# An RWKV block cut into 37 paced steps in place of 31, and eight small predicated copies into two

## The chip, the cores and the metric

The kernel runs on one core of a Trainium2 chip. What is compared is the device time of one execution in microseconds, the median over several runs. The engines are TensorE (PE, matrix products; its weight loads are listed as PEld), VectorE (DVE), ScalarE (ACT), GpSimd (POOL) and SyncE (SP, which only starts transfers here).

## What is computed

One layer of a hybrid network runs over 2048 prompt rows and 32 sample rows of width 1024: a modulated norm, one projection to 3464 columns, three kinds of heads side by side on those columns, an output projection, and a feed-forward part. All is float32; a large product is made of three products of rounded parts. The change lies in the first kind of heads, RWKV-7, four heads of width 64, whose state S is carried along the rows:

```python
def step(S, inp):
    r_t, k_t, v_t, kk_t, a_t, w_t = inp
    s_kk = jnp.einsum('bhvk,bhk->bhv', S, kk_t)
    S = (S * w_t[:, :, None, :] - s_kk[..., None] * (kk_t * a_t)[:, :, None, :]
         + v_t[..., None] * k_t[:, :, None, :])
    return S, jnp.einsum('bhvk,bhk->bhv', S, r_t)
```

Before it stand elementwise operations on the projected columns (decay w, gate a, a normalized kk); after it come a norm by head, a bonus term and a gate. The other two kinds are HGRN2 (four heads, a gated recurrence) and forgetting attention (eight heads).

## The kernel before

The first part of the program, `project_and_recur` (L1956), does three things at once: the large projection, the RWKV recurrence and the HGRN2 recurrence. The projection is `cm_cols` and `tm_cols` of `InProj`: groups of 24 matmuls into a PSUM tile `ip_p` (L378 to L380, L409 to L411). It does not depend on the recurrences, and it is what PE has to do while they wait for other engines.

The RWKV rows are taken in 16 blocks of 128 rows, and one of 64 for the sample: 17 blocks, each a generator `rwkv_block` (L1097) that yields after each step. A block turns the recurrence into products within chunks of 64 rows. Its steps, with the names that return below:

- loads and token shift, decay and gate (`rw_ga`), the norm of kk by a product with `bones` (L1161, "the bones product") and the operations after it;
- the operands: `G` (L1171 to L1174) and `kb` (L1175 to L1182), eight operations on DVE and one on POOL, all in one step;
- the products of `G` and `kb` (L1189, "the kb product"), masked on DVE into `gm` (L1193), one half copied by ACT into `m0` (L1197);
- the first level of a triangular inverse `tt`: eight predicated copies (L1219, which are recorded at L1015 in the helper `by_level`), a transpose to `tn` (L1220), and in the same step the transpose of v on PE, copied by ACT to `rw_wu` (L1223);
- the product `nv` of `gm` and `rw_wu` (L1229);
- five more levels (h = 2 to 32), each of two half steps: PE, then ACT (`rw_x`, L1258); PE, then DVE (predicated copy, transpose L1267);
- products with the inverse, the two chunk states `rw_s`, the output `rw_y`, its norm, and its store to `yT`, a transfer started from ACT's queue (L1344).

The order of the program's instructions is written by `interleave` (L2105): it always advances the generator with the least position. A block starts every 1.0, and each of its yields moves it on by `RW_LEN / RW_STEPS`. So a step is 1.5/31 = 0.0484 of a block's start distance, and blocks overlap. `coupled` (L2093) advances an HGRN2 block by 0.65 of a step at each RWKV step. The projection's generator advances by its own measure beside them. The products of the two recurrences go through `small` (L222), which puts them ahead of projection matmuls that are ready and fixes their order against them. How many projection matmuls stand on PE between two products of a block is thus set by the number of yields between them. An engine takes its instructions in the order in which they stand.

After the last block the rest of the projection goes on beside attention; the output projection and the feed-forward part follow.

Of the kernel before, what the change touches and what calls it, by code (L numbers as in the profile page):

```python
# [1003 lines left out]
def halves(t, h, u):  # L1004

    return t.rearrange("p (b u x) -> p b u x", u=2, x=h)[:, :, u, :]


def by_level(K, dst, h, src, rows=slice(0, 128)):

    n, b, x = dst.shape[1] // 64, 32 // h, h
    m = K.lev_up[h][rows].bitcast(mybir.dt.uint32).rearrange("p (b x) -> p b x", x=h)
    m = m[:, None, :, :].broadcast_to([m.shape[0], n, b, x])
    d = dst.rearrange("p (c b u x) -> p c b u x", c=n, u=2, x=h)[:, :, :, 1, :]
    K.nc.vector.copy_predicated(d, m, src)  # L1015
# [81 lines left out]
def rwkv_block(K, rp, pp, t0, T, n, first, st):  # L1097
# [5 lines left out]
    NK, W = 2 * C, 2 * T  # L1103
# [33 lines left out]
    for j in range(2):  # L1137
# [5 lines left out]
    sq = tmp()  # L1143
    nc.scalar.activation(sq, kk, AF.Square)
    yield


    b = sb("rw_b")
# [23 lines left out]
    nc.vector.tensor_tensor(G[:, 1], ch(xr), ch(w), ALU.mult)  # L1172
    nc.gpsimd.tensor_tensor(G[:, 2], K.i2[:, None, :].broadcast_to([128, NK, 64]), ends.broadcast_to([128, NK, 64]),
                            ALU.mult)  # L1174
    kb = rp.tile([128, NK, 2, 64], F32, name="rw_kb", bufs=KB)  # L1175
    nc.vector.scalar_tensor_tensor(kk, kk, -1.0, av, ALU.mult, ALU.mult)
    nc.vector.tensor_tensor(kb[:, :, 1, :], ch(kk), ch(wi), ALU.mult)
    kp = av
    for j in range(2):
        nc.vector.tensor_scalar(kp[:, js[j]], av[:, js[j]], vec(K, "rw_k_a", j), K.ka1[:, j:j + 1], ALU.mult, ALU.add)  # L1180
    nc.vector.tensor_tensor(kp, kp, xk, ALU.mult)
    nc.vector.tensor_tensor(kb[:, :, 0, :], ch(kp), ch(wi), ALU.mult)  # L1182

    yield

    gm, gps = [], [pt() for _ in hs]
# [4 lines left out]
    for ps in gps:  # L1191
        g = rp.tile([128, NK, 192], F32, name=f"rw_gm{len(gm)}", bufs=GM)
        nc.vector.tensor_tensor(g[:, :, 0:128], ps[:, :128 * NK].rearrange("p (k x) -> p k x", x=128), mask, ALU.mult)  # L1193
        gm.append(g)
        if len(gm) == 1:
            m0 = rp.tile([64, NK, 64], F32, name="rw_m0", bufs=1)
            nc.scalar.activation(m0, g[64:, :, 0:64], AF.Copy)  # L1197
    yield

    kf = kb.rearrange("p k a t -> p k (a t)")  # L1200
# [3 lines left out]
    tt = rp.tile([128, NK, 64], F32, name="rw_tt", bufs=TT)  # L1204
    tn = rp.tile([128, NK, 64], F32, name="rw_tn", bufs=1)
    wu = rp.tile([128, 2, NK, 2, 64], F32, name="rw_wu", bufs=WU)
    flat = lambda t: t.rearrange("p k t -> p (k t)")

    def tokens(src):

        ps = pt()
        for j in range(2):
            transpose(ps[:T, 128 * j:128 * j + 128], src[:, C * j:C * j + C, :], K.ident)
        return [ps[64 * c:64 * c + 64, :256].rearrange("p (j h x) -> p j h x", j=2, h=2) for c in range(C)]

    nc.gpsimd.tensor_copy(tt, K.i2[:, None, :].broadcast_to([128, NK, 64]))
    for h, m in zip(hs, mt):
        for k in range(NK):
            by_level(K, tt[h, k, :], 1, halves(m[:, k, :], 1, 1)[:, None], h)  # L1219
    nc.vector.transpose(tn, tt)  # L1220

    for c, v in enumerate(tokens(ch(xv))):
        nc.scalar.activation(wu[:64].rearrange("p h (j c) a x -> p c a j h x", j=2)[:, c, 1], v, AF.Copy)  # L1223
    yield

    nv = pt()
# [136 lines left out]
class Rwkv:  # L1363
# [13 lines left out]
    def block(self, t0):  # L1377
        first = 0 if t0 == 0 else None
        return rwkv_block(self.K, self.rp, self.pp, t0, self.T, self.T, first, self.st)
# [16 lines left out]
    def sample(self):  # L1396
        K, rp, pp, nc = self.K, self.rp, self.pp, self.K.nc
        s0 = rp.tile([128, 2, 64], F32, name="rw_z", bufs=1)
        nc.sync.dma_start(out=s0, in_=K.a["state_rwkv"][0, 0].rearrange("(j h) v k -> (h v) j k", j=2))
        ps = pp.tile([128, 512], F32, name="rw_ps")  # L1400
        for p in range(2):
            for h in (slice(0, 64), slice(64, 128)):
                nc.tensor.matmul(ps[h, 64 * p:64 * p + 64], lhsT=s0[h, p, :], rhs=K.i2[h, :], start=True, stop=True)
        s = rp.tile([128, 2, 64], F32, name="rw_zs", bufs=1)
        nc.scalar.activation(s, ps[:, :128].rearrange("p (j x) -> p j x", j=2), AF.Copy)
        st = [s]
        yield from rwkv_block(K, rp, pp, SEQ, 64, NS, 1, st)
        self.out(st[0], K.o["rw_state_sample"])
# [678 lines left out]
        yield from K.fx.run([(h, 0) for h in range(8)], 512, 4, K.banks, FX_LEAD0)  # L2087


RW_LEN, RW_STEPS, HG_STEP, IP_LEAD = 1.5, 31, 0.65, 0.5  # L2090


def coupled(main, other, steps):  # L2093
# [133 lines left out]
```

## Time and profile before

| | |
|---|---|
| median of 3 runs (lowest to highest) | 3648.11 us (3646.69 to 3655.67) |
| profiled execution, its own time | 3646.97 us |
| span of its trace | 3645.3 us |
| PE busy | 3416.8 us, 94% |
| DVE, ACT, POOL busy | 52%, 38%, 38% |
| mean granted TensorE clock | 0.972 |

Busy time counts an engine from an instruction's start to its end. PE is busy nearly always, so what is to be had is in its gaps and in stretches where its clock is granted at less than full speed. The first recurrence product starts at about 168 us, the last at 1254.7 us.

### The profile page before, as it was taken

To read this page: it belongs to the slowest core of one execution; us is meant where nothing else is said; L and a number is where in the kernel's file an instruction comes from. 1 tells how busy PE (TensorE), PEld (TensorE's weight loads), DVE (VectorE), ACT (ScalarE), POOL (GpSimd) and SP (SyncE) were. 2 spreads that over 40 slices of the span, in tenths; PEclk is the share of its full clock that TensorE was granted. 3 is DMA by queue.
4 is the path that set the end of the run, shared out by engine and by line. 5 is a ranking of instruction groups with operands and counts; after the bars stand their busy time and mean duration, and the time that the engine had idled before them with its cause. 6 is when DMAs were issued, how large, how long until landed. Compare 5 with 4: busy or idle time off the path is not lost.

```text
span 3645.3 us, 61001 instructions
## 1 busy us (share of the span) xinstructions
PE 3416.8 (94%) x24106; PEld 2877.2 (79%) x24106; DVE 1890.9 (52%) x3953; ACT 1399.7 (38%) x2865; POOL 1382.2 (38%) x1458
## 2 busy tenths in 40 slices
PE   7998899989899998999999999899999999999999
PEld 5988788878777875666666666688999998998998
DVE  3456656575657565656666665532333344233336
ACT  4345556455455453544443443322122213211212
POOL 5424444443334413644443443333223333322223
PEclk9999999999989998999999999999999999999999
DMA  6433334324542344322222214533222232211212
GB/s 213 144 111 100 93 115 128 122 79 142 173 133 67 119 140 126 122 69 66 60 80 59 75 50 107 178 128 100 64 64 76 70 95 98 70 58 47 70 58 96
DMA packets 362482, 361.25 MB, mean 99 GB/s; under 512 B 35359, under 2 KB 304244, under 8 KB 361140
## 3 DMA queue, kind: packets, MB, share of 16 engines
q1 hardware_dynamic: 324336, 320.02, 28.8%
q10 hardware_dynamic: 37476, 37.29, 3.3%
q8 instruction: 189, 3.10, 0.4%
q14 instruction: 97, 0.79, 0.1%
q0 software_dynamic: 384, 0.05, 0.0%
HBM read 291.14 MB, written 66.14 MB: 98 GB/s over the span
## 4 chain that ended last, share of the span: by engine, by line
PE 58%; DVE 5%; POOL 4%; issue 3%; DMA 2%; ACT 2%; ACTq 0%; POOLq 0%; SPq 0%; DVEq 0%
PE ff_p L1878 8%; PE ff_p L1879 8%; PE ff_p L1877 8%; PE ff_o L1828 4%; PE ff_o L1829 4%; PE ff_o L1827 4%; PE pb_pv L712 4%; PE pb_sc L665 2%; PE pb_ps L728 2%; PE rw_ps L227 2%; POOL fx_acc L722 2%; PE pb_ps L729 1%; PE op_p L1737 1%; PE op_p L1735 1%; PE op_p L1736 1%
## 5 line engine op out<-in xcount | busy, mean ns | idle before, releaser
L1878 PE MATMUL ff_p<-h_lo,wih 128*128 128x384 f32 (+2 forms) x1760 | 622.7, 354 | 0.2 <-POOL h_lo L1952 0.2
L1877 PE MATMUL ff_p<-h_hi,wih 128*128 128x384 f32 (+2 forms) x1760 | 621.2, 353 | 1.1 <-DVE op_r L1739 0.4
L1879 PE MATMUL ff_p<-h_hi,wil 128*128 128x384 f32 (+2 forms) x1760 | 620.9, 353 | 1.1 <-POOL wil L1764 1.1
L1764 POOL TENSOR_TENSOR wil<-ff_st,wih 128x1024 fp32r<-128x1024 f32 x134 | 322.0, 2403 | 578.9 <-ACT wih L1763 540.2
L378 PE MATMUL ip_p<-h_hi,w_hi 128*128 128x256 f32 (+1 forms) x1472 | 458.9, 312 | 19.4 <-ACT ip_e L345 6.6
L379 PE MATMUL ip_p<-h_lo,w_hi 128*128 128x256 f32 (+1 forms) x1472 | 428.9, 292 | 6.7 <-POOL h_lo L203 3.6
L380 PE MATMUL ip_p<-h_hi,w_lo 128*128 128x256 f32 (+1 forms) x1472 | 427.0, 290 | 0.0
L1877 PEld LDWEIGHTS ff_p<-h_hi,wih 128*128 128x128 f32 x1760 | 331.3, 188 | 17.2 <-issue 0.9
L1879 PEld LDWEIGHTS ff_p<-h_hi,wil 128*128 128x128 f32 x1760 | 332.9, 189 | 14.2 <-POOL wil L1764 1.4
L1878 PEld LDWEIGHTS ff_p<-h_lo,wih 128*128 128x128 f32 x1760 | 331.4, 188 | 14.5 <-POOL h_lo L1952 0.6
L378 PEld LDWEIGHTS ip_p<-h_hi,w_hi 128*128 128x128 f32 x1472 | 284.7, 194 | 50.6 <-issue 19.0
L1764 POOL TENSOR_TENSOR wol<-ff_st,woh 128x1024 fp32r<-128x1024 f32 x66 | 161.3, 2449 | 408.0 <-ACT woh L1763 408.0
L722 POOL TENSOR_TENSOR fx_acc<-fx_acc,fx_pt 128x512 f32<-128x512 f32 (+3 forms) x176 | 209.1, 1203 | 274.0 <-PE pb_pv L712 157.1
L1886 DVE TENSOR_TENSOR ff_sg<-ff_sg,ff_p 128x384 f32<-128x384 f32 (+2 forms) x110 | 64.5, 586 | 461.7 <-PE ff_p L1879 457.0
L1833 DVE TENSOR_TENSOR acc<-acc,ff_o 128x512 f32<-128x512 f32 (+1 forms) x306 | 208.8, 684 | 173.6 <-PE ff_o L1829 173.0
L379 PEld LDWEIGHTS ip_p<-h_lo,w_hi 128*128 128x128 f32 x1472 | 286.1, 194 | 14.4 <-POOL h_lo L203 4.7
L1827 PE MATMUL ff_o<-woh,act_h 128*128 128x512 f32 (+1 forms) x724 | 286.9, 396 | 10.3 <-ACT act_h L1887 7.6
L380 PEld LDWEIGHTS ip_p<-h_hi,w_lo 128*128 128x128 f32 x1472 | 285.0, 194 | 3.9 <-issue 2.4
L1829 PE MATMUL ff_o<-woh,act_l 128*128 128x512 f32 (+1 forms) x724 | 287.7, 398 | 0.0
L1828 PE MATMUL ff_o<-wol,act_h 128*128 128x512 f32 (+1 forms) x724 | 286.9, 396 | 0.0
L1763 ACT ACTIVATE wih<-ff_st 128x1024 fp32r<-128x1024 f32 x134 | 142.0, 1060 | 362.4 <-PE ff_p L1878 315.9
L336 POOL TENSOR_TENSOR w_lo<-w_st,w_hi 128x256 fp32r<-128x256 f32 (+2 forms) x220 | 163.2, 771 | 179.8 <-ACT w_hi L334 161.8
(450 smaller groups left out, 7085.7 us busy)
## 6 DMA issues: line engine op xcount, KB each, us to landing
ff_st<-w_ffn_in SPq DMA_DIRECT2D x132, 512.0 KB
w_st<-w_in SPq DMA_DIRECT2D x88, 512.0 KB
ff_st<-w_ffn_out SPq DMA_DIRECT2D x68, 512.0 KB
cm<-ip_e SPq DMA_DIRECT2D x92, 256.0 KB
x_t<-w_ada SPq DMA_DIRECT2D x32, 512.0 KB
fx_kr<-cm SPq DMA_DIRECT2D x80, 128.0 KB
w_st<-w_in SPq DMA_DIRECT2D x16, 520.0 KB
w_a<-w_ada SPq DMA_DIRECT2D x8, 1024.0 KB
```

The source lines that it names most:

```text
L378: nc.tensor.matmul(ps[:, :T], lhsT=whi[:, d, us], rhs=S.hi[:, d, :T], start=(d == 0), stop=False)
L379: nc.tensor.matmul(ps[:, :T], lhsT=whi[:, d, us], rhs=S.lo[:, d, :T], start=False, stop=False)
L380: K.behind[1:] = [nc.tensor.matmul(ps[:, :T], lhsT=wlo[:, d, us], rhs=S.hi[:, d, :T], start=False, stop=(d == ND - 1))]
L722: eng.tensor_tensor(acc[i % 2][:m, c0:nq], acc[i % 2][:m, c0:nq], pt[:m, c0:nq], ALU.add)
L1764: nc.gpsimd.tensor_tensor(lo, st, f32(hi), ALU.subtract)
L1827: nc.tensor.matmul(ps[:m], lhsT=ah[:, js], rhs=wh[:, cs], start=(n == 0), stop=False)
L1828: nc.tensor.matmul(ps[:m], lhsT=ah[:, js], rhs=wl[:, cs], start=False, stop=False)
L1829: nc.tensor.matmul(ps[:m], lhsT=al[:, js], rhs=wh[:, cs], start=False, stop=(n == 1))
L1833: nc.vector.tensor_tensor(acc[j][:m, cs], acc[j][:m, cs], ps[:m], ALU.add)
L1877: nc.tensor.matmul(ps[:, :S], lhsT=w[0][:, ds], rhs=hh[:, d, :S], start=(d == 0), stop=False)
L1878: nc.tensor.matmul(ps[:, :S], lhsT=w[0][:, ds], rhs=hl[:, d, :S], start=False, stop=False)
L1879: nc.tensor.matmul(ps[:, :S], lhsT=w[1][:, ds], rhs=hh[:, d, :S], start=False, stop=(d == ND - 1))
```

## The change

Six more `yield`s are put into `rwkv_block`: an empty step after kk, three between the operands and the kb product (`G` / one half of `kb` / the other half / an empty step), one empty step after `gm`, one after the step with `rw_wu`. The eight predicated copies of the first level, for each half of the partitions one for each of four pieces of 64 columns, become one copy for each half. The pace goes from 31 steps in 1.5 to 37 in 1.6, and HGRN2 advances by 0.6 per step.

```diff
     sq = tmp()
     nc.scalar.activation(sq, kk, AF.Square)
     yield
+    yield
...
     nc.gpsimd.tensor_tensor(G[:, 2], K.i2[:, None, :].broadcast_to([128, NK, 64]), ends.broadcast_to([128, NK, 64]),
                             ALU.mult)
+    yield
     kb = rp.tile([128, NK, 2, 64], F32, name="rw_kb", bufs=KB)
     nc.vector.scalar_tensor_tensor(kk, kk, -1.0, av, ALU.mult, ALU.mult)
     nc.vector.tensor_tensor(kb[:, :, 1, :], ch(kk), ch(wi), ALU.mult)
+    yield
     kp = av
     for j in range(2):
         nc.vector.tensor_scalar(kp[:, js[j]], av[:, js[j]], vec(K, "rw_k_a", j), K.ka1[:, j:j + 1], ALU.mult, ALU.add)
     nc.vector.tensor_tensor(kp, kp, xk, ALU.mult)
     nc.vector.tensor_tensor(kb[:, :, 0, :], ch(kp), ch(wi), ALU.mult)
-
+    yield
     yield
...
             m0 = rp.tile([64, NK, 64], F32, name="rw_m0", bufs=1)
             nc.scalar.activation(m0, g[64:, :, 0:64], AF.Copy)
     yield
+    yield
...
     for h, m in zip(hs, mt):
-        for k in range(NK):
-            by_level(K, tt[h, k, :], 1, halves(m[:, k, :], 1, 1)[:, None], h)
+        by_level(K, flat(tt)[h], 1, m.rearrange("p k (b u x) -> p k b u x", u=2, x=1)[:, :, :, 1, :], h)
     nc.vector.transpose(tn, tt)
 
     for c, v in enumerate(tokens(ch(xv))):
         nc.scalar.activation(wu[:64].rearrange("p h (j c) a x -> p c a j h x", j=2)[:, c, 1], v, AF.Copy)
     yield
+    yield
...
-RW_LEN, RW_STEPS, HG_STEP, IP_LEAD = 1.5, 31, 0.65, 0.5
+RW_LEN, RW_STEPS, HG_STEP, IP_LEAD = 1.6, 37, 0.6, 0.5
```

The change moves instructions on every engine. Two places are shown, both of the 13th block. The first is PE, from the kb product to the product nv. Before, with the last row shown the first nv product:

```order
L227 MATMUL rw_ps<-rw_G,rw_kb 128x128 x8
L227 MATMUL rw_ps<-ident,rw_v 128x128 x2
L378 MATMUL ip_p<-h_hi,w_hi 128x256
L379 MATMUL ip_p<-h_lo,w_hi 128x256
L380 MATMUL ip_p<-h_hi,w_lo 128x256
L195 MATMUL nt_ps<-ident,xn 128x128 x3
L227 MATMUL rw_ps<-rw_wu,rw_gm_13046 64x64
```

Now, in the middle of the same stretch (the transpose of v, between projection matmuls):

```order
L378 MATMUL ip_p<-h_hi,w_hi 128x256
L379 MATMUL ip_p<-h_lo,w_hi 128x256
L380 MATMUL ip_p<-h_hi,w_lo 128x256
L227 MATMUL rw_ps<-ident,rw_v 128x128 x2
L227 MATMUL hg_ps<-hg_x 64x96 x8
L378 MATMUL ip_p<-h_hi,w_hi 128x256
```

From the kb product to the transpose of v there are now 12 projection matmuls (the first three rows shown are the last of them), and from there to nv 12 more. Before there were none and 3, so 24 stand where 3 stood.

The second place is ACT, around the copy of v to `rw_wu`. Before:

```order
L334 ACTIVATE w_hi<-w_st 128x4x256 x2
L1344 DMA yT<-rw_y 128x2x128
L1076 ACTIVATE rl_e<-rl_e,lsc 128x128
L1223 ACTIVATE rw_wu<-rw_ps 64x2x2x64 x2
L1197 ACTIVATE rw_m_13048<-rw_gm_13046 64x256
```

Now (the lines have moved by 3 or 4):

```order
L1348 DMA yT<-rw_y 128x2x128
L345 ACTIVATE ip_e<-ip_p 128x256
L1200 ACTIVATE rw_m_13042<-rw_gm_13040 64x256
L1226 ACTIVATE rw_wu<-rw_ps 64x2x2x64 x2
L201 ACTIVATE h_hi<-h_t 128x4x128
```

The store of the block before, which waits for POOL's `rw_y`, stands ahead of `rw_wu` in both; the copy to `m0` now stands between, and nv is 24 projection matmuls from the kb product in place of 3.

## Rows read from the trace of the kernel before

**Rows 1.** The page's head and its part 1.

```profile
span 3645.3 us, 61001 instructions
...
PE 3416.8 (94%) x24106; PEld 2877.2 (79%) x24106; DVE 1890.9 (52%) x3953; ACT 1399.7 (38%) x2865; POOL 1382.2 (38%) x1458
```

**Rows 2.** Windows, the recurrence stage: busy by engine, granted clock, DMA share, GB/s.

```profile
160.00:1255.00 1095.00, 1005.62 (x11453) 887.34 (x11453) 680.97 (x1913) 575.64 (x1479) 458.99 (x751) 0.96 0.38 115
```

**Rows 3.** Waits of PE, 160 to 1255 us: total us, times, longest.

```profile
PE rw_ps L227 <- DVE rw_kb L1182: 20.3, 14, 3.5
PE rw_ps L227 <- ACT rw_wu L1223: 10.8, 7, 2.4
PE rw_ps L227 <- DVE rw_gm L1193: 10.3, 5, 3.6
...
PE rw_ps L227 <- DVE w_lo L336: 3.7, 1, 3.7
...
PE rw_ps L227 <- DVE rw_tn L1267: 2.3, 2, 2.1
...
PE rw_ps L227 <- ACT rw_x L1258: 2.1, 4, 0.7
```

**Rows 4.** Waits of PE, 160 to 970 us (blocks 1 to 12).

```profile
PE rw_ps L227 <- DVE rw_kb L1182: 15.0, 10, 3.5
```

**Rows 5.** Waits of PE, 970 to 1255 us (blocks 13 to 17).

```profile
PE rw_ps L227 <- DVE rw_kb L1182: 5.3, 4, 3.0
```

**Rows 6.** Windows of 20 us behind seven long waits; the granted clock stands third last.

```profile
322.00:342.00 20.00, 17.55 (x213) 15.97 (x212) 13.77 (x45) 10.60 (x33) 6.44 (x14) 0.91 0.36 93
452.00:472.00 20.00, 17.53 (x160) 16.23 (x161) 9.53 (x39) 7.51 (x32) 5.67 (x22) 0.91 0.26 72
517.00:537.00 20.00, 16.52 (x187) 15.20 (x187) 15.24 (x47) 7.69 (x19) 7.60 (x13) 0.91 0.55 165
860.00:880.00 20.00, 17.06 (x217) 15.13 (x219) 14.46 (x46) 9.02 (x30) 4.88 (x8) 0.91 0.40 117
989.00:1009.00 20.00, 16.41 (x175) 14.60 (x174) 13.35 (x42) 7.17 (x22) 7.61 (x11) 0.66 0.27 81
1056.00:1076.00 20.00, 18.37 (x178) 16.35 (x180) 13.63 (x48) 6.84 (x22) 6.67 (x9) 0.57 0.35 104
1214.00:1234.00 20.00, 17.96 (x212) 15.98 (x213) 8.57 (x31) 7.03 (x25) 2.91 (x3) 0.83 0.19 62
```

**Rows 7.** Timeline of PE around the kb product of block 14: start, us, instruction.

```profile
1054.21 0.28 PE L380 MATMUL ip_p<-h_hi,w_lo 128*128 128x256 f32 x1
1054.33 0.28 PE L378 MATMUL ip_p<-h_hi,w_hi 128*128 128x256 f32 x1
1057.63 2.08 PE L227 MATMUL rw_ps<-rw_G,rw_kb 64*128 64x128 f32 x16 [3.03 <-DVE rw_kb L1182]
...
1060.34 0.41 PE L380 MATMUL ip_p<-h_hi,w_lo 128*128 128x256 f32 x1
1060.56 0.41 PE L378 MATMUL ip_p<-h_hi,w_hi 128*128 128x256 f32 x1
```

**Rows 8.** Timeline of DVE ahead of that product.

```profile
1055.29 1.37 DVE L198 TENSOR_SCALAR h_t<-nt_ps,s_norm,sh_norm 128x128 f32<-128x128 f32 x4 [4.34 <-POOL h_lo L203]
```

**Rows 9.** Timeline of ACT at the nv product of block 17.

```profile
1216.83 0.38 ACT L1223 ACTIVATE rw_wu<-rw_ps 64x256 f32<-64x256 f32 x1 [3.49 <-POOL rw_y L1343]
```

**Rows 10.** Waits of DVE, 160 to 1255 us.

```profile
DVE rw_tt L1015 <- PE rw_ps L227: 113.6, 68, 6.1
```

**Rows 11.** Groups of DVE by line and form, 160 to 1255 us: predicated copies.

```profile
L1015 DVE COPY_PREDICATED rw_tt<-lev_up,rw_ps 128x128 f32<-128x128 uint32 x80 | 26.1, 327 | 106.2 <-PE rw_ps L227 106.1
...
L1015 DVE COPY_PREDICATED rw_tt<-lev_up,rw_m 64x32 f32<-64x32 uint32 x66 | 14.5, 302 | 9.2 <-ACT rw_m L1197 9.2
...
L1015 DVE COPY_PREDICATED rw_tt<-lev_up,rw_gm 64x32 f32<-64x32 uint32 x66 | 10.2, 244 | 0.2
```

**Rows 12.** Timeline of DVE at the last operand of block 6 (kb product at 520.64 us).

```profile
520.16 0.42 DVE L1182 TENSOR_TENSOR rw_kb<-rw_ga,rw_b 128x256 f32<-128x256 f32 x1
```

## Prediction

> **What bounds the kernel now.** I read the page's part 1 first. PE is busy for 3416.8 of 3645.3 us [rows 1], so every engine but PE works beside it, and time is gained only where PE stands still or runs slowly. The change touches the recurrence stage, 160 to 1255 us. The windows view gives that stage 1005.6 us of PE in 1095, so 89.4 us of idle time, at a granted clock of 0.96 [rows 2]. Four hundredths of 1095 us are 44 us of lost PE work, half as much as the gaps cost. DVE, the next engine, has 681 us of work in the stage [rows 2], 62%: it isn't the bound of the whole stage, only of short stretches.
>
> The waits of PE say where the gaps are. The kb product waited 20.3 us for DVE's last operand, in 14 places. The next product, nv, waited 10.8 us for ACT's `rw_wu`, 10.3 us for DVE's `gm` and 3.7 us for a DVE operation in front of it [rows 3]. Together that is 45.1 us in 27 places, half of the idle time of the stage. All of it lies in front of two products of a block's first part. The levels, ten half steps in each of 17 blocks, wait almost nowhere: 2.3 us on `rw_tn` and 2.1 us on `rw_x` [rows 3]. Instead DVE stands and waits for a level's product in 68 places, 113.6 us [rows 10], which means that at the levels PE comes last.
>
> The timeline shows what a wait costs. Before the kb product of block 14 PE stops for 3.03 us; before the stop, projection matmuls start every 0.12 us, after it every 0.22 us [rows 7]. That is the clock at its lower level, 1.2 in place of 2.4 GHz. Seven windows of 20 us behind long waits of these two products have granted clocks of 0.91 (four times), 0.66, 0.57 and 0.83 [rows 6]. The missing shares times 20 us are 1.8 four times, 6.8, 8.6 and 3.4: 26.0 us. So the two products cost 45.1 + 26.0 = 71.1 us, which is the most that the change could give if nothing else got worse.
>
> **The sum, part by part.** It is made against the profiled execution, 3646.97 us, which is 1.1 us under the median of the runs; its span is 1.7 us less.
>
> *The cover of the first part.* In the built order I counted projection matmuls between the products of each block. From the kb product to nv there were 3 to 30 in each block; now there are 12 in block 14 and 24 to 102 in the others. At 0.12 us [rows 7] the usual 24 to 60 are 2.9 to 7.2 us, against single waits of at most 3.6 us [rows 3]. So the nv waits go, apart from block 14: of 24.8 us I take 22. A second cause of theirs weakens too: ACT reached `rw_wu` of block 17 after standing 3.49 us behind the store of the block before, which waits for POOL's `rw_y` [rows 9]. The store is still ahead of it, but nv now comes later.
>
> From the bones product to the kb product there were 24 to 51 matmuls in blocks 1 to 12, leaving out block 6, where the count is disturbed, and there are now 42 to 66. In blocks 13 to 17 there were 29 to 70 and there are 27 to 54: no more than before. So I let the 15.0 us of blocks 1 to 12 [rows 4] fall by 13, and the 5.3 us of the last five [rows 5] by 1. What is late in block 14 is not the amount of work for the operands: DVE stood 4.34 us at a norm operation that waited for POOL's `h_lo` [rows 8], with the rest of the operands queued behind it. In the new order such a norm operation still stands in front of them.
>
> *The clock.* Of the 26.0 us I leave the 8.6 of block 14 in place. The other 17.4 go where the waits go; I take 14.
>
> *The first level.* Eight copies, four of 302 and four of 244 ns [rows 11], are 2.18 us a block; two copies of 128 elements cost at most the 327 ns of the form with twice the partitions [rows 11], 0.65 us. The difference of 1.5 us a block is 26 us of DVE, beside other work: PE's cover is the nv product and the matmuls around it. I book nothing for it. If that cover went, the 1.5 us would be what it gives.
>
> *The shorter steps.* A step falls from 0.0484 to 0.0432 of a block's distance, 11%. Where no `yield` was put in, less stands between two products. From the first level to the product with the inverse I counted 1864 projection matmuls over 17 blocks, and 1673 now: 191 fewer, 22.9 us at 0.12 us. That is the upper bound of what the levels can lose in cover; the lower is nothing, and the waits of 4.4 us on the levels today are nearest to nothing. I take 5 us, and two more falls of the clock at 1.8 us as in the common window [rows 6], 3.6 us.
>
> *The rest.* A block now lasts 34 steps of 0.0432, 1.47 distances, in place of 28 of 0.0484, 1.36; so the next block's first steps lie beside the last levels. HGRN2's pace changes by 3%. The operations on POOL and the stores on ACT's queue that sit in moved steps are needed no sooner than before. After the last RWKV product 312 projection matmuls are left in place of 330, so 18 × 0.12 = 2 us of PE work change sides. PE's 44 us of other idle time (89.4 - 45.1) meets engines that must do the same work in less time: I add 6 us, an eighth. Its bounds are nothing and the 44 us once more.
>
> The sum: 22 + 13 + 1 + 14 = 50 us gained, 5 + 3.6 + 6 = 14.6 us given back, 35 us net. **3647 - 35 = 3612 us.**
>
> **Rivals.**
>
> *The blocked queue.* Waits come from one late operation at the head of DVE's or ACT's queue, and not from how little stands between two products. For it: rows 8 and 9 are just that, and in the new order the operands are mixed with as many operations of HGRN2 and of the norm as before. Against it: before the kb product of block 6, which waited longest, DVE's last operand follows without idle time [rows 12], so there the work itself is late; and cover helps against either cause. If half of the 50 us stays, the result is 25 - 14.6 = 10 us, 3636; with a mild form, where a third stays, it is 3628. I take 3632 for this case. The Trainium skill, "TensorE: Matmul & The Clock Gate", in the section on the array's architectural detail, states that ScalarE and VectorE keep strictly to the order of their queues, and that PE alone pulls something ahead, its weight loads. By that rule the operands behind the norm operation had to wait, as the trace shows with its 4.34 us [rows 8], and splitting their step leaves that queue what it is.
>
> *No change to be seen.* PE comes earlier to other places and waits there: HGRN2's products, the norms, the weights of the next group. Then the 50 us are matched by the second bound of the rest, 44 us, and the levels' 8.6: 3647 + 2.6, about 3650. Against it: DVE has 38% of the stage free, ACT and POOL more [rows 2].
>
> *Slower: the levels become the bound.* Each half step has less between its products, and the next block's first operations now fall beside the last levels. If one half step in every block comes late as the waits of today do, it costs 45.1/27 = 1.7 us and one fall of the clock, 1.8 us: 17 × 3.5 = 60 us. With all 22.9 us of lost cover on the path besides, and the gain of 50 in full, the result is 3647 + 60 + 23 - 50 = 3680. It decides from 50/3.5, some 14 late half steps of 170, on. Against it: DVE waits for PE at 68 level products and not the other way round [rows 10].
>
> **How the numbers follow.** I give the forecast 0.62, the blocked queue 0.19, no change 0.10, slower 0.09. Some 0.3%, 11 us, is what a measurement of this kernel can tell from no change. The forecast lies beyond it, and the blocked queue mostly (0.17 of its 0.19), so faster has 0.79; within 0.3%: 0.10 + 0.02 = 0.12; slower 0.09. If the whole 71.1 us went and nothing were given back, 3576 would result; I hold that for rare and begin the range at 3588, which is the 50 us and most of the clock of block 14 with nothing given back. Its upper end, 3640, takes in the forecast with the levels at their 22.9 us and the blocked queue. What lies above is no change and slower, 0.19 together, less what of them falls below 3640.
>
> **What would show it.** In the changed kernel's waits of PE the kb product should stand at 5 to 8 us and nv (`rw_wu`, `gm`) below 5 us in all, with the granted clock of the stage at 0.97 to 0.98 and its end near 1220 us. The waits of the levels should stay below 12 us. The blocked queue would show as kb and nv waits above 20 us with DVE idle in front; the slower case as `rw_tn` and `rw_x` waits above 40 us. The forecast is wrong if the stage's idle time stays above 75 us, or if the time after the stage, where the order of instructions differs only around the first attention work, moves by more than 10 us.

## The result and the profile after

The changed kernel takes 3606.05 us (median of 4 runs, 3603.43 to 3616.27); the kernel before, timed with it, 3647.99 us. The ratio is 0.9886, 95% interval 0.9862 to 0.9910. The forecast was 3612, the range 3588 to 3640. The profiled execution took 3604.76 us.

The page's head and part 1 of the changed kernel answer to [rows 1]:

```profile
span 3603.0 us, 60961 instructions
...
PE 3408.2 (95%) x24106; PEld 2859.4 (79%) x24106; DVE 1883.4 (52%) x3855; ACT 1403.1 (39%) x2865; POOL 1371.8 (38%) x1458
```

These two lines split the gain. Span less busy time is PE's idle time: 228.5 us before [rows 1], 194.8 now, so 33.7 less. The number of matmuls is the same, 24106, and their busy time is 8.6 less: they ran less at the lower clock. 33.7 + 8.6 = 42.3 us, the fall of the span. The same split is used for every run below, with one caution: idle time repeats well from execution to execution, busy time less so. The kernel before and e1 below, which is as fast, have nearly the same idle time (228.5 and 226.9), but e1 has 9.1 us more of busy time, and most of that lies behind the recurrence stage, where the two programs do the same work:

```profile
1255.00:3645.00 2390.00, 2281.78 (x11713) 1874.94 (x11713) 1148.84 (x1887) 760.42 (x1274) 849.39 (x530) 0.98 0.28 86
1253.00:3652.00 2399.00, 2291.00 (x11712) 1881.49 (x11710) 1146.72 (x1887) 761.77 (x1274) 849.15 (x530) 0.97 0.29 86
```

Those are windows of the kernel before and of e1, PE's busy time in the third column. From 160 to 1255 us the two have 1005.6 and 1006.7 us. So a difference in busy time of the whole span is trusted only beyond some 9 us, one within the stage sooner.

Windows of the changed kernel, columns as in [rows 2]: the old stretch, the stage up to its new end, and 20 us behind the kb product of block 14:

```profile
160.00:1255.00 1095.00, 1032.79 (x11780) 904.00 (x11780) 701.16 (x1892) 603.76 (x1534) 465.40 (x783) 0.98 0.40 122
160.00:1208.00 1048.00, 990.85 (x11481) 866.98 (x11482) 675.42 (x1818) 583.07 (x1490) 450.40 (x753) 0.98 0.40 121
...
1018.00:1038.00 20.00, 17.61 (x263) 15.61 (x264) 14.99 (x44) 12.51 (x44) 6.82 (x11) 1.00 0.44 129
```

The last state product starts at 1207.62 us (third row of the next block), before at 1254.23 (its fourth row): 46.6 us of gain lie in the stage, and 4.3 are lost behind it, which is less than the kernel before and e1 differ by there. Up to the new end PE is idle for 57.2 us (89.4 before [rows 2]) at a clock of 0.98 (0.96).

Timeline of PE at the kb product of block 14, the last state product, and the last state product of the kernel before:

```profile
1016.03 0.28 PE L380 MATMUL ip_p<-h_hi,w_lo 128*128 128x256 f32 x1
1018.86 1.16 PE L227 MATMUL rw_ps<-rw_G,rw_kb 64*128 64x128 f32 x16 [2.55 <-DVE rw_kb L1185]
...
1207.62 0.68 PE L227 MATMUL rw_ps<-rw_G,rw_s 64*64 64x64 f32 x16
1254.23 0.68 PE L227 MATMUL rw_ps<-rw_G,rw_s 64*64 64x64 f32 x16
```

Waits of PE in the changed kernel, 160 to 1255 us (total us, times, longest), to be held against [rows 3]:

```profile
PE rw_ps L227 <- ACT rw_wu L1282: 9.2, 8, 2.8
PE hg_ps L227 <- DVE hg_att L1493: 8.3, 7, 1.9
PE ip_p L378 <- DVE ip_e L343: 6.5, 3, 5.1
PE rw_ps L227 <- ACT rw_t L1330: 5.7, 7, 2.1
PE nt_ps L124 <- DMA x_t<-w_ada: 4.9, 4, 2.3
PE rw_ps L227 <- ACT rw_x L1262: 4.3, 4, 2.0
PE nt_ps L195 <- DVE h_t L198: 3.7, 2, 2.1
PE rw_ps L227 <- DVE rw_tn L1271: 3.1, 5, 1.2
PE rw_ps L227 <- DVE rw_kb L1185: 3.1, 2, 2.6
```

The kb product waits 3.1 us in 2 places; it was 20.3 in 14. The nv product's `rw_wu` (now L1226) and `gm` (L1196) are not in the list at all; they were 21.1 us, with `w_lo` 24.8. The `rw_wu` that is there, L1282, is a later copy, for the products with the inverse. The list is now flat: no wait above 10 us. For what grew, these are the waits of the kernel before that [rows 3] leave out:

```profile
PE hg_ps L227 <- DVE hg_x L1474: 6.7, 3, 3.8
...
PE rw_ps L227 <- ACT rw_wu L1278: 3.5, 5, 1.9
...
PE hg_ps L227 <- DVE hg_att L1489: 2.3, 1, 2.3
...
PE rw_ps L227 <- ACT rw_t L1326: 0.8, 2, 0.4
```

The groups of DVE by line and form show the two copies that take the place of eight [rows 11], in 16 of the 17 blocks:

```profile
L1015 DVE COPY_PREDICATED rw_tt<-lev_up,rw_gm 64x128 f32<-64x128 uint32 x16 | 9.2, 575 | 0.5
...
L1015 DVE COPY_PREDICATED rw_tt<-lev_up,rw_m 64x128 f32<-64x128 uint32 x16 | 8.4, 526 | 1.3 <-ACT rw_m L1200 1.3
```

The waits of DVE in the same stretch, against [rows 10]:

```profile
DVE rw_tt L1015 <- PE rw_ps L227: 101.0, 58, 7.5
```

Two copies cost 1.10 us a block, not the 0.65 that the prediction allowed at most; they save 1.1 us of 2.18. And DVE still waits for PE at the levels, in 58 places.

### The profile page after: what moved, and what is told of

Read it like the earlier page. It is cut to its first block, busy times and chain, and to the rows that moved or that the text cites. A ratio compares the mean times of both kernels' runs of the same rounds, so it can differ in the third digit from the quotient of the medians.

```text
span 3603.0 us, 60961 instructions
## 1 busy us (share of the span) xinstructions
PE 3408.2 (95%) x24106; PEld 2859.4 (79%) x24106; DVE 1883.4 (52%) x3855; ACT 1403.1 (39%) x2865; POOL 1371.8 (38%) x1458
## 4 chain that ended last, share of the span: by engine, by line
PE 61%; DVE 6%; POOL 4%; ACT 3%; DMA 3%; issue 3%; ACTq 0%; SPq 0%; POOLq 0%; DVEq 0%
PE ff_p L1883 8%; PE ff_p L1882 8%; PE ff_p L1881 8%; PE ff_o L1832 4%; PE ff_o L1833 4%; PE ff_o L1831 4%; PE pb_pv L712 4%; PE rw_ps L227 3%; PE pb_sc L665 2%; PE pb_ps L728 2%; PE op_p L1740 1%; PE op_p L1739 1%; PE op_p L1741 1%; PE pb_ps L729 1%; PE ip_p L378 1%
## 5 line engine op out<-in xcount | busy, mean ns | idle before, releaser
L1883 PEld LDWEIGHTS ff_p<-h_hi,wil 128*128 128x128 f32 x1760 | 333.0, 189 | 14.4 <-POOL wil L1768 1.4
L1882 PEld LDWEIGHTS ff_p<-h_lo,wih 128*128 128x128 f32 x1760 | 331.8, 188 | 14.4 <-POOL h_lo L1956 0.6
```

What stands on the lines that cost most here:

```text
L1882: nc.tensor.matmul(ps[:, :S], lhsT=w[0][:, ds], rhs=hl[:, d, :S], start=False, stop=False)
L1883: nc.tensor.matmul(ps[:, :S], lhsT=w[1][:, ds], rhs=hh[:, d, :S], start=False, stop=(d == ND - 1))
```

## The experiments

Four explanations were set against each other: the *cover* (more projection matmuls stand between a block's products), the *queue* (waits come from what stands ahead of the late operation on DVE or ACT), the *copies* (DVE's chain is shorter), and the *length* (a block lasts longer and overlaps the next differently). Idle is the span less PE's busy time on each page, as above.

| kernel | median us | ratio to before [95%] | idle us | busy us |
|---|---|---|---|---|
| changed kernel | 3606.05 | 0.9886 [0.9862, 0.9910] | 194.8 | 3408.2 |
| e1, copies alone | 3654.14 | 1.0005 [0.9992, 1.0018] | 226.9 | 3425.9 |
| e2, change without copies | 3611.00 | 0.9891 [0.9872, 0.9911] | 203.6 | 3405.6 |
| e3, operands split alone | 3608.54 | 0.9886 [0.9864, 0.9909] | 200.2 | 3407.7 |
| e4, steps before nv alone | 3621.29 | 0.9914 [0.9894, 0.9934] | 207.8 | 3405.7 |
| e5, change at the old pace | 3593.30 | 0.9837 [0.9812, 0.9862] | 188.8 | 3402.6 |
| e6, new pace alone | 3686.78 | 1.0086 [1.0059, 1.0113] | 242.8 | 3447.3 |
| e7, longer block alone | 3653.05 | 1.0000 [0.9985, 1.0015] | 230.6 | 3421.3 |
| e9, store on SP's queue | 3645.90 | 0.9982 [0.9968, 0.9996] | 226.1 | 3419.5 |
| e10, change, still longer | 3611.06 | 0.9873 [0.9851, 0.9894] | 206.1 | 3409.5 |
| e11, e5 with a step in HGRN2 | 3635.28 | 0.9949 [0.9930, 0.9967] | 220.3 | 3409.4 |
| e12, e3 and e4 together | 3607.14 | 0.9882 [0.9868, 0.9897] | 198.1 | 3408.8 |
| e13, e5 with HGRN2 faster | 3637.98 | 0.9971 [0.9954, 0.9989] | 209.7 | 3420.6 |

The kernel before was timed anew beside each group of runs (medians 3647 to 3654 us), so ratios are compared, not medians.

**e1 and e2: the copies.** e1 is the kernel before with this edit alone; e2 is the changed kernel with the edit taken back.

```diff
-        for k in range(NK):
-            by_level(K, tt[h, k, :], 1, halves(m[:, k, :], 1, 1)[:, None], h)
+        by_level(K, flat(tt)[h], 1, m.rearrange("p k (b u x) -> p k b u x", u=2, x=1)[:, :, :, 1, :], h)
```

> The kernel before with the two predicated copies alone; steps and pace stay at 31 in 1.5. Theory A (the gain is cover put in front of the kb product and of nv): DVE loses some 25 us of work, but PE's waits on rw_kb stay near 20 us and those on rw_wu and gm near 21; time within 8 us of 3647. Theory B (the gain is DVE work taken out of a crowded first part): kb and nv waits fall by half or more, time 3632 or less.

> The changed kernel with the eight copies of the first level put back; all yields and the new pace stay. Theory A: kb waits near 3 us, nv waits below 3 us, time 3603 to 3614, as the changed kernel's 3606. Theory B: half of the gain goes, 3625 or more, with new waits on gm or on the first level's rw_tn.

e1 gives 1.0005, and its kb wait is 20.1 us in 15 places, as before. e2 gives 0.9891, which its interval does not set apart from the whole change. So no worth of the copies can be seen in either surrounding, as booked: DVE's saved microsecond lies beside PE's other work. A few us within the change are not excluded; e2 has 8.8 us more idle time than the changed kernel.

**e3 and e4: each half of the cover alone**, at the old step length. e3 has the three `yield`s among the operands, e4 the two around nv.

```diff
+    yield
     kb = rp.tile([128, NK, 2, 64], F32, name="rw_kb", bufs=KB)
...
+    yield
     kp = av
...
-
+    yield
     yield
...
-RW_LEN, RW_STEPS, HG_STEP, IP_LEAD = 1.5, 31, 0.65, 0.5
+RW_LEN, RW_STEPS, HG_STEP, IP_LEAD = 1.5 * 34 / 31, 34, 0.65, 0.5
```

```diff
             nc.scalar.activation(m0, g[64:, :, 0:64], AF.Copy)
     yield
+    yield
...
         nc.scalar.activation(wu[:64].rearrange("p h (j c) a x -> p c a j h x", j=2)[:, c, 1], v, AF.Copy)
     yield
+    yield
...
-RW_LEN, RW_STEPS, HG_STEP, IP_LEAD = 1.5, 31, 0.65, 0.5
+RW_LEN, RW_STEPS, HG_STEP, IP_LEAD = 1.5 * 33 / 31, 33, 0.65, 0.5
```

> The kernel before with the three yields between the operands and the kb product alone, 34 steps at the old step length (0.0484), HGRN2 at 0.65 per step. Theory A: kb waits fall from 20 us below 6, nv waits stay at 15 to 25 us; half-speed time falls by a part; time 3620 to 3632. Theory C (a late queue behind DVE or ACT, whatever stands between): kb waits stay above 12 us and time stays within 8 us of 3647.

> The kernel before with the two empty steps around nv alone (after gm, and after the transpose of v), 33 steps at the old step length, HGRN2 at 0.65 per step. Theory A: waits on rw_wu L1223, gm and the DVE operation ahead of nv fall from 24.8 us below 4, kb waits stay at 15 to 25 us; time 3612 to 3626. Theory C: nv waits stay above 12 us, time within 8 us of 3647.

Waits of PE in e3, same stretch and columns:

```profile
PE rw_ps L227 <- ACT rw_wu L1225: 14.4, 12, 2.3
PE rw_ps L227 <- ACT rw_wu L1280: 11.4, 10, 2.3
...
PE hg_ps L227 <- DVE hg_att L1491: 1.8, 2, 1.0
```

Waits of PE in e4:

```profile
PE rw_ps L227 <- DVE rw_kb L1182: 15.1, 13, 2.5
```

Each edit removes the wait that it stands in front of and leaves more than half of the other: in e3 the kb product's 20.3 us are gone but for one stop of 2.9, while nv's `rw_wu` (L1225) is there with 14.4 us of nv's 24.8 (the wait on `gm` is gone as well); in e4 nv is gone and kb is there with 15.1. That speaks for the cover, place by place. But e3 alone gives 0.9886, all that the whole change gives and more than was expected of it, and e4 alone 0.9914; the two intervals overlap. The halves don't add up. In both the granted clock from 160 to 1255 us is 0.98, as in the changed kernel (0.96 before), and busy time falls by 9.1 and 11.1 us: either half alone gives back as much of the clock as the whole change.

**e5 and e6: the pace.** e5 is the changed kernel with the old step length (1.5/31 of a block's distance) and HGRN2's 0.65; e6 is the kernel before with the new numbers alone.

```diff
-RW_LEN, RW_STEPS, HG_STEP, IP_LEAD = 1.6, 37, 0.6, 0.5
+RW_LEN, RW_STEPS, HG_STEP, IP_LEAD = 1.5 * 37 / 31, 37, 0.65, 0.5
```

```diff
-RW_LEN, RW_STEPS, HG_STEP, IP_LEAD = 1.5, 31, 0.65, 0.5
+RW_LEN, RW_STEPS, HG_STEP, IP_LEAD = 1.6, 37, 0.6, 0.5
```

> The changed kernel at the old step length: 37 steps in 1.5*37/31 = 1.79 (0.0484 a step), HGRN2 at 0.65 per step. Theory A, with my price for shorter steps (8.6 us on the levels): level waits fall back to some 5 us from 8.7, time 3595 to 3604. Theory F (both parts of the cover buy the same thing, so more of it is worth nothing): 3603 to 3615.

> The kernel before at the new pace (37 in 1.6, HGRN2 at 0.6), no yield added: each step is 11% shorter and a block lasts 1.21 of a start distance instead of 1.36. Theory A: less cover, kb and nv waits grow by some 10% to 30%, time 3650 to 3670. Theory D (what helps is another phase of the blocks against each other and against the norms, whatever it is): time 3635 or less.

The page of e6, its head and part 1:

```profile
span 3690.1 us, 61094 instructions
...
PE 3447.3 (93%) x24106; PEld 2894.4 (78%) x24106; DVE 1892.5 (51%) x3953; ACT 1396.2 (38%) x2865; POOL 1381.0 (37%) x1458
```

Its waits of PE, 160 to 1255 us:

```profile
PE rw_ps L227 <- DVE rw_kb L1182: 41.5, 17, 5.7
PE rw_ps L227 <- DVE rw_gm L1193: 10.2, 9, 3.0
```

With shorter steps and no `yield` added the kb wait doubles, from 20.3 to 41.5 us, now in 17 places, and the kernel is slower by 0.9%, some 31 us, more than was expected. No operation was added anywhere; less stands in front of the product. (The order on DVE moves with the pace too, so e6 alone does not part cover from queue.) The window of e6's stage, up to its last state product, columns as in [rows 2]:

```profile
160.00:1278.00 1118.00, 1015.81 (x11448) 893.29 (x11449) 689.19 (x1913) 574.42 (x1485) 458.09 (x750) 0.95 0.37 112
```

The stage is 23 us longer than before, 12.8 of idle and 10.2 of busy time: here the clock costs nearly as much as the stops. Over the whole span idle time rises by 14.3 us and busy time by 30.5; two thirds of that busy time lie outside the stage, and the profiled execution is the second slowest of five (3674.19 to 3696.03 us), so they are not counted as a price of the pace. At this same pace the `yield`s and copies of the change are worth 1.0086 - 0.9886, 2.0% or some 73 us.

e5 is the best version, 0.9837, and beats both kernels. Its page:

```profile
span 3591.4 us, 60926 instructions
...
PE 3402.6 (95%) x24106; PEld 2864.6 (80%) x24106; DVE 1870.6 (52%) x3855; ACT 1396.8 (39%) x2865; POOL 1372.6 (38%) x1458
```

Its waits of PE, 160 to 1255 us:

```profile
PE hg_ps L227 <- ACT hg_t L1094: 8.1, 8, 1.6
```

The span is 11.6 us under that of the changed kernel, 6.0 of idle and 5.6 of busy time; by the ratios it is 0.49%, some 18 us. The two intervals meet at 0.9862, and the slowest run of e5, 3599.94 us, is faster than the fastest of the changed kernel, 3603.43. So the new pace is a cost within the change. It has two parts that e5 undoes together: steps 11% shorter, and HGRN2 3.3% faster (0.6 × 37/1.6 = 13.88 of its steps per block start in place of 0.65 × 31/1.5 = 13.43).

**e7, e9 and e10: length and queue.** e7 makes the block longer with three empty steps ahead of its last one, where nothing waits; e9 takes the store of `yT`, behind which ACT stood in [rows 9], off ACT's queue; e10 gives the changed kernel longer steps still.

```diff
     yield
+    yield
+    yield
+    yield
     nc.gpsimd.tensor_tensor(y, y, t2, ALU.add)
...
-RW_LEN, RW_STEPS, HG_STEP, IP_LEAD = 1.5, 31, 0.65, 0.5
+RW_LEN, RW_STEPS, HG_STEP, IP_LEAD = 1.5 * 34 / 31, 34, 0.65, 0.5
```

```diff
-    nc.scalar.dma_start(out=K.yT[0:256, t0:t0 + n].rearrange("(j p) t -> p j t", p=128), in_=pairs(y)[:, :, :n])
+    nc.sync.dma_start(out=K.yT[0:256, t0:t0 + n].rearrange("(j p) t -> p j t", p=128), in_=pairs(y)[:, :, :n])
```

```diff
-RW_LEN, RW_STEPS, HG_STEP, IP_LEAD = 1.6, 37, 0.6, 0.5
+RW_LEN, RW_STEPS, HG_STEP, IP_LEAD = 2.0, 37, 0.72, 0.5
```

> The kernel before with three empty steps ahead of a block's last step, 34 steps at the old step length, HGRN2 at 0.65: a block lasts as long as with the operand split alone, the store of a block moves behind the next block's nv, but nothing more stands in front of the kb product or nv. Theory A: kb waits stay at 16 to 24 us; nv waits on rw_wu fall only where the store caused them; time 3632 to 3648. Theory D (the length of a block and its phase make the gain of the two halves): kb waits below 12 us, time 3625 or less.

> The kernel before with the store of RWKV's output started from SP's queue in place of ACT's, nothing else. If the store's wait for POOL in ACT's queue makes the nv waits: waits on rw_wu L1223 fall from 10.8 to below 4 us, kb waits stay at 20, gm waits at 10, time 3632 to 3645. If not: rw_wu waits stay above 8 us and time within 8 us of 3647. Slower than 3655 if SP's loads queue behind the store.

> The changed kernel with still longer steps: 37 in 2.0 (0.0541 a step against 0.0484 of the kernel at the old step length and 0.0432 of the change), HGRN2 at 0.72 so that its pace stays. If cover is still what is missing: level waits below 3 us, idle time of the stage below 45 us, 3580 to 3590. If the cover is now enough, or a block of 1.84 start distances meets its single buffers (rw_wu, kept until the output): 3593 to 3610, with waits on the release of buffers. Against 3593 of the old step length.

The first line of e7's waits of PE, 160 to 1255 us:

```profile
PE rw_ps L227 <- DVE rw_kb L1182: 19.8, 14, 3.7
```

e7 gives 1.0000, with kb at 19.8 us: the same three steps that gave 1.1% among the operands give nothing at the end, so length is not the cause. e9 gives 0.9982: nv's two waits fall from 21.1 to 14.8 us, but the time falls by 0.2%; its `rw_wu` wait, 7.1 us, lies between the two cases that had been set against each other. So the store in ACT's queue is a small part at most. The operation that held DVE's queue in block 14 [rows 8] was taken out in no run. e10 gives 0.9873, no better than the changed kernel and by its median worse than e5, though their intervals overlap; idle time is 206.1 us, with HGRN2's `hg_w` (10.7 us) and the levels' `rw_tn` (10.5 us) at the head of the waits. More cover, given in this form, does not go on helping.

**e11, e12 and e13: what is left.** e12 is the changed kernel without the empty step after kk and with the eight copies, at the old step length; so it holds the edits of e3 and e4. e11 and e13 try to shorten e5's `hg_t` wait: e13 advances HGRN2 by 0.70 for each step, e11 does that and adds an empty step in the HGRN2 block. A block of HGRN2 has 13 steps, so in e11 it lasts 14/0.70 = 20 RWKV steps, as in e5 (13/0.65), and in e13 18.6.

Of e12 (the copies as in e1, turned round), e11 and e13, against the changed kernel:

```diff
     yield
-    yield
...
-RW_LEN, RW_STEPS, HG_STEP, IP_LEAD = 1.6, 37, 0.6, 0.5
+RW_LEN, RW_STEPS, HG_STEP, IP_LEAD = 1.5 * 36 / 31, 36, 0.65, 0.5
```

```diff
         yield
+    yield
     ps = pt()
...
-RW_LEN, RW_STEPS, HG_STEP, IP_LEAD = 1.6, 37, 0.6, 0.5
+RW_LEN, RW_STEPS, HG_STEP, IP_LEAD = 1.5 * 37 / 31, 37, 0.7, 0.5
```

```diff
-RW_LEN, RW_STEPS, HG_STEP, IP_LEAD = 1.6, 37, 0.6, 0.5
+RW_LEN, RW_STEPS, HG_STEP, IP_LEAD = 1.5 * 37 / 31, 37, 0.7, 0.5
```

> The changed kernel at the old step length (3593) with one empty step in HGRN2 behind the transposes of its values and keys, HGRN2 at 0.70 per step. If cover works there as it does in RWKV: the waits of HGRN2's products on ACT's hg_t fall from 8.1 us below 3, time 3583 to 3591. If those waits are late for another reason: hg_t waits above 5 us and 3589 to 3600.

> The kernel before with the operand split and the two empty steps around nv together, at the old step length (36 steps in 1.5*36/31), HGRN2 at 0.65; the step after kk and the two copies of the change are left out. Alone the two parts gave 41 and 31 us. If they add up: 3574 to 3584. If they partly buy the same waits, as their half-speed time suggests (44 us of it left in either, from 96): 3590 to 3606; near 3593 the step after kk and the copies are worth nothing.

> The changed kernel at the old step length (3593) with HGRN2 at 0.70 per step and no step added to it. If the pace of HGRN2 against RWKV made the 42 us that the kernel with a step more in HGRN2 lost: 3620 or more, with waits on rw_wu L1282 and rw_x near 10 us each. If the added step made them: 3588 to 3602.

Waits of PE in e12:

```profile
PE hg_ps L227 <- DVE hg_att L1493: 10.7, 9, 2.5
PE hg_ps L227 <- DVE hg_x L1478: 6.1, 3, 4.7
PE rw_ps L227 <- ACT rw_wu L1282: 5.2, 5, 1.8
```

With both halves the nv waits are gone from its list, kb is down to one of 1.1 us, and the time is that of e3, 0.9882. What the second half frees is lost again, and the list says where most of it went: HGRN2's products wait for DVE, 16.8 us in two lines, where e3 had 1.8 for `hg_att` and 0.4 for `hg_x`.

Waits of PE in e13, 160 to 1255 us:

```profile
PE rw_ps L227 <- ACT rw_wu L1282: 9.2, 14, 1.7
PE rw_ps L227 <- DVE rw_tn L1271: 9.1, 8, 2.5
PE hg_ps L227 <- ACT hg_t L1094: 7.4, 9, 1.3
```

Waits of PE in e11:

```profile
PE rw_ps L227 <- ACT rw_wu L1282: 11.5, 14, 2.6
PE rw_ps L227 <- ACT rw_x L1262: 10.4, 12, 2.3
```

Both e11 and e13 are slower than e5; e11 lies outside both times expected of it, e13's time came as expected for the case that the pace costs. HGRN2's steps 7.7% closer together make e13's span 38.9 us longer than e5's, 20.9 idle and 18.0 busy, and `hg_t` still waits 7.4 us. In e11 the `hg_t` wait is not in the list any more, so the added step covers its product as in RWKV; yet e11 is as slow as e13, with RWKV's `rw_wu` and `rw_x` at the head of the waits. So the added step does not make the loss, and since a block of HGRN2 lasts as long in e11 as in e5, an earlier end of the block does not either; the shorter distance of HGRN2's steps is what both share.

## Why the prediction was right, point by point

**The cover: right, and somewhat larger.** Of the 45.1 us of kb and nv waits 36 were to go; 42.0 went. Blocks 1 to 12 and nv did as said; their longest single wait had been 3.7 us [rows 3] and not the 3.6 of the prediction, on which nothing hangs. In the last five blocks kb fell from 5.3 to 2.6 us where only 1 had been booked. e6 (less cover, 41.5 us), e3 and e4 (each place by itself) and e7 (steps elsewhere, nothing) show that it is the cover and neither length nor, with e1 and e2, the copies. Whether the late operation is late by its own work or by what stands ahead of it in its queue they do not part: cover helps against either, as the prediction said.

**Block 14: half right.** Its stop stayed, 2.55 us for 3.03 [rows 7], and for the cause given: DVE stood 3.40 us for POOL's `h_lo` (4.34 in [rows 8]) with the operands behind. The timeline of DVE in the changed kernel:

```profile
1015.70 1.36 DVE L198 TENSOR_SCALAR h_t<-nt_ps,s_norm,sh_norm 128x128 f32<-128x128 f32 x4 [3.40 <-POOL h_lo L203]
1016.98 0.59 DVE L1184 TENSOR_TENSOR rw_ga<-rw_ga,rw_k 128x256 f32<-128x256 f32 x1
```

The Trainium skill, "TensorE: Matmul & The Clock Gate", section on architectural detail, states that ScalarE and VectorE keep strictly to the order of their queues; that row agrees with it. But the 8.6 us of clock that the prediction left in place behind this stop did not stay: the granted clock of the 20 us behind it is 1.00, where it was 0.57 [rows 6].

**What is given back: right in size, wrong in place.** Idle time in the stage outside the kb and nv waits was 89.4 - 45.1 = 44.3 us and is 57.2 - 3.1 = 54.1: 9.8 more, with 11 booked (5 at the levels, 6 elsewhere). The levels took 3.0 (`rw_x` and `rw_tn`, 4.4 to 7.4). The largest rises stand at `rw_wu` L1282 (3.5 to 9.2), `hg_att` (2.3 to 8.3) and `rw_t` (0.8 to 5.7), while others fell, `hg_x` from 6.7 us to nothing. So idle time in the stage fell by 32.2 us for 25 forecast.

**The clock: the right sign, too small in the stage, near in total by luck.** 14 less 3.6, 10.4 us, were booked. PE's busy time fell by 14.8 us up to the last state product (1005.62 to 990.85), although 28 more matmuls lie there, and rose by 6.2 in the rest. That rise is within what the kernel before and e1 differ by behind the stage, so the net 8.6 is not a measure of the forecast.

**The parts and the total.** That the halves do not add up is what the sum could not see: it priced the clock per stop, and e3 and e4 each give back all of it. Alone e3 was expected to give 15 to 27 us and gave some 41, e4 21 to 35 and gave some 31; together, in e12, they give some 43. The sum added the parts, each by its own wait, and booked little for the pace; that its total came within 6 us of the result is in part luck.

**The pace: undervalued as an edit, its parts still open.** The sum had 5 + 3.6 us for shorter steps. As an edit of its own the new pace costs 31 us (e6), within the change 18 by the ratios and 11.6 by the two spans (e5 against it). HGRN2's 3% was named without a price of its own, and e13 makes that doubtful: 7.7% cost 0.0134 of the ratio there, so 3.3% would in proportion be 0.0057, an estimate, as much as the whole 0.0049 between e5 and the changed kernel. It may be the shorter steps, HGRN2's pace, or both; neither was put back alone.

**The rivals.** The blocked queue asked for kb and nv waits above 20 us; there are 3.1. The slower case asked for 40 us at the levels; there are 7.4. That nothing changes is excluded by the interval of the ratio. Of the signs named, stage clock 0.98 and levels below 12 us came as said, the time behind the stage moved by 4.3 us (under 10); kb came lower than 5 to 8, and the stage ended at 1208 and not near 1220.

**Open.** e5 is 0.45% faster than e12, from which it differs by the empty step after kk and the copies; e1 and e2 make the copies unlikely, but the step was not tried alone. Why HGRN2's pace weighs so much was not found.

## What to carry to other kernels

Where an interleaver hands out cover by steps, put the empty steps in front of the products that wait, and do not change the pace of the steps, or of another interleaved chain, in the same edit: here that gave a fifth to a third of the possible gain away (42 us of span in place of 54, or 1.1% in place of 1.6). Add one place at a time, since the next waiter takes over: here one of the two places already gave all that both gave. Split each result into idle and busy time of the engine that bounds the kernel; that tells stops from clock. Take both from the stage that the edit touches, since over the whole span busy time differs by some 9 us between executions of equally fast kernels.

## What was unexpected of the hardware

A stop has no fixed price in clock. Behind the kb product of block 14 the granted clock of 20 us was 0.57 after a stop of 3.03 us and 1.00 after one of 2.55 at the same place of the program. Within the stage, e6 lost 10.2 us of busy time beside 12.8 of idle time, and the change won 14.8 beside 32.2. The copy of the first level had a bound that did not hold: 64x128 elements took 526 and 575 ns, where 128x128, twice the partitions, takes 327 at the other levels [rows 11]. What in its operands makes the difference was not tried.
